# Silu on ScalarE for the gate, and six Strassen groups of inner columns instead of seven, spread over longer stretches

## The chip, the cores and the metric

The kernel runs on one core of a Trainium2 chip. The metric is device time in microseconds, as the median of three runs: 1667.15 us before the change, and the three runs lay between 1666.97 and 1667.17 us. TensorE (PE) multiplies matrices into PSUM, with a separate weight load before each matmul (PEld). VectorE (DVE) and ScalarE (ACT) do elementwise work, each in the order in which its instructions stand. SyncE (SP) issues the DMA transfers that bring the weights.

## What is computed

One decoder layer in fp32 with 256 tokens and a model width of 2048: two token mixers side by side, then a feed-forward part whose inner width is 5632.

```python
D_FF = ((8 * D_MODEL // 3 + 255) // 256) * 256          # 5632, eleven groups of 512
...
h = h + mixed @ w_out[l]
hn = rmsnorm(h, norm2_w[l])
h = h + (jax.nn.silu(hn @ w_gate[l]) * (hn @ w_up[l])) @ w_down[l]
return rmsnorm(h, norm_f_w)
```

`silu(z)` is `z * sigmoid(z)`. The change concerns only the line with `silu`: the gate, up and down projections.

## The kernel before

**Three products for one.** Every fp32 operand is split into a rounded part and a remainder, `hi` and `lo`, and a product is computed as `hi*hi + lo*hi + hi*lo`. For each weight tile ACT writes `hi` (line 169) and DVE subtracts it from the raw tile to get `lo` (line 170). So each weight that PE uses has passed ACT and DVE first.

**Units.** The work is a list of units, each with one weight tile. A plain unit (lines 300 to 331) loads 128x2048 numbers, 1 MB, and makes 24 matmuls with 512 columns at line 315. A pair unit (`strassen`, lines 334 to 385) loads 128x1024 numbers, 0.5 MB, of which DVE makes three more slots by subtraction (lines 187 to 189); ACT and DVE split seven slots, 128x1792, and PE makes 21 matmuls with 256 columns at line 362. This is Strassen's scheme with seven products in place of eight. It saves PE columns and costs DVE work.

**Groups.** The inner width is cut into eleven groups of 512 columns. A plain group is eight plain units: four for the gate (`wg`) and four for the up projection (`wu`). A Strassen group is sixteen pair units: eight for the gate (`sg`) and eight for up (`su`). Each set of eight pair units sums into the four PSUM banks of the pool `sp`, and `finish` (lines 374 to 383) forms the result `Z` out of them with one ACT copy and four DVE additions (lines 376 to 382). `PLAIN` (line 44) lists four plain groups, and the other seven are Strassen groups.

**Gate, up and turn.** When a gate's sums are ready, ACT takes the sigmoid (line 1160) and DVE multiplies it by the scaled gate (line 1161), for each of two token chunks. When up is ready, DVE multiplies by it (line 1165). Then `turn` transposes the product on PE (line 1180), and ACT and DVE split it into `f` (lines 1183, 1184), which is the operand of the down projection.

**Down.** Four parts, `PARTS`, take three, three, three and two groups. A part's four column blocks are twelve plain units (eight in the last part), `wd`; DVE adds their sums to `y` (line 1222).

**Order.** `ROW` (line 49) is a list of steps. Each names a main list of plain units (a plain group, or a down part) and the Strassen groups whose pair units `spread` (line 402) lays between the main units, evenly, with none behind the last `tail` main units. Only the last step with Strassen units has a tail, of 3. `run_units` (line 205) goes through the list, loads up to three units ahead, and there are three `hi` and `lo` buffers and four raw buffers in this phase (`WBUFS`, line 53, and one more each from line 1060). The DVE order is that of the program from unit 30 on (`manual_schedule`, line 1260). PE and ACT are reordered by the scheduler when the program is built, so parts of neighbouring units can change places there.

Of the kernel before, what the change touches and what calls it, by code (L numbers as in the profile page):

```python
# [9 lines left out]
AF = mybir.ActivationFunctionType  # L10
ALU = mybir.AluOpType
# [29 lines left out]
DLY, STEP = 1, 2  # L41

PARTS = [(0, 3), (3, 6), (6, 9), (9, 11)]
PLAIN = [0, 2, 5, 8]
NGRP = 11
STD = [4 * g + i for g in PLAIN for i in range(4)]
SGRP = [4 * g for g in range(NGRP) if g not in PLAIN]

ROW = [(("group", 0), [1]), (("group", 2), [3]), (("down", 0), [4]), (("group", 5), [6]), (("down", 1), [7]),
       (("group", 8), [9]), (("down", 2), [10]), (("down", 3), [])]  # L50


WBUFS = dict(raw=3, hi=2, lo=2)
# [13 lines left out]
def kernel(  # L67
# [991 lines left out]
    with tc.tile_pool(name="ffn", bufs=1) as ffn:  # L1059
# [92 lines left out]
        def group(g):  # L1152

            H = {}

            def gate(c, z):
                if c == 0:
                    H["sg"] = ffn.tile([P, 4, S], F32, tag="sg", name=f"sg_g{g}", bufs=2)
                v = H["sg"][:, 2 * c:2 * c + 2]
                A_.activation(v, z, AF.Sigmoid, scale=rt2[:, c:c + 1])  # L1160
                V.scalar_tensor_tensor(out=v, in0=z, scalar=rt2[:, c:c + 1], in1=v, op0=ALU.mult, op1=ALU.mult)

            def up(c, z):
                v = H["sg"][:, 2 * c:2 * c + 2]
                V.scalar_tensor_tensor(out=v, in0=z, scalar=rt2[:, c:c + 1], in1=v, op0=ALU.mult, op1=ALU.mult)
                if c == NC - 1:
                    if may_turn(g):
                        after(1, turn)
                    else:
                        turns.append((g, turn))  # L1170

            def turn():
                fh, fl = get_f(part_of[g])
                sg = H["sg"].rearrange("p a b -> p (a b)")
                for m in range(2):
                    ps = ps_unit(f"ptr_g{g}_{m}")
                    for i in range(2):
                        f = (2 * m + i) * P
                        for c in range(NC):
                            PE.transpose(out=ps[:, i * S + c * P:i * S + (c + 1) * P],  # L1180
                                         in_=sg[:, 2 * c * S + f:2 * c * S + f + P], identity=ident)
                    j = 4 * (g - PARTS[part_of[g]][0]) + 2 * m
                    A_.activation(flat(fh[:, j:j + 2]), ps, AF.Copy)
                    V.tensor_tensor(out=flat(fl[:, j:j + 2]), in0=ps, in1=flat(fh[:, j:j + 2]).bitcast(F32),  # L1184
                                    op=ALU.subtract)
                turned.append(g)
            return gate, up
# [21 lines left out]
            return (strassen(wst[i, 0], (hh, hl, sh, sl), z_tiles, f"sg{g}", then(gate, False)) +  # L1209
                    strassen(wst[i, 1], (hh, hl, sh, sl), z_tiles, f"su{g}", then(up, True)))  # L1210

        def down(pi):
            g0, g1 = PARTS[pi]

            def operand(g):
# [3 lines left out]
            def evac(q):  # L1219
# [14 lines left out]
                        downs[0] += 1  # L1234
                        run_turns()
                return fn
            for q in range(4):
                token_major_tiles(lambda g, q=q: wdown[4 * q:4 * q + 4, :, 512 * g:512 * g + 512], operand,
                                  range(g0, g1), f"wd{pi}_{q}", evac(q), ps_unit, by_chunk=(pi == last and q == 3))

        def listed(make):
            n = len(units)
            make()
            got = units[n:]
            del units[n:]
            return got
# [2 lines left out]
        dgf = ffn.tile([P, NC, P], F32, name="dgf")  # L1249
        for f in range(KT):  # L1250
            feature_major(wout[f], KT, mh, ml, f"wo{f}", wo_evac(f))
        for (kind, n), sides in ROW:
            main = listed(lambda: (plain_group if kind == "group" else down)(n))
            units.extend(spread(main, sum((strassen_group(g) for g in sides), []), 0, 3 if NGRP - 1 in sides else 0))
        find_free()
        load_next()
        with tc.issue_after(mm["last"]):
# [116 lines left out]
```

## Time and profile before

| | |
|---|---|
| median of three runs | 1667.15 us |
| profiled execution | 1667.3 us |
| its span, first to last instruction | 1665.5 us |
| granted TensorE clock | 0.997 of 2.4 GHz over the span |
| first matmul of the first plain group | 915.6 us |
| first matmul of the first down part | 1091.6 us |
| last sums leave, output part begins | 1652.4 us |

The feed-forward part thus takes 736.8 us of the span, and everything before 915.6 us has the same instructions on PE before and after. In the profile "busy" of an engine is the time in which some instruction of it is on record. Matmuls overlap, and a matmul's record lasts longer than the distance to the next one's start, so PE can be on record as busy through a short stall. The distance between starts in a long run of equal matmuls is the better measure of what PE needs.

The steps of `ROW` are told below by the time at which PE starts each step's first plain matmul: 915.6, 999.7, 1091.6, 1201.5, 1288.2, 1402.4 and 1489.9 us. They are called the first to the seventh old stretch. Stretches 1, 2, 4 and 6 have a plain group of eight main units, stretches 3, 5 and 7 a down part of twelve. The last down part stands behind the seventh, to 1652.4 us; in the windows below the two are divided at 1595 us.

### The profile page before, as it was taken

The numbers are of one execution on the slowest core, as the hardware profiler recorded it, in microseconds if no ns is written. First come the engines' busy times: TensorE is split into PE (matmuls) and PEld (weight loads), VectorE is DVE, ScalarE is ACT, GpSimd is POOL, SyncE is SP. The second block draws the span as 40 slices with busy tenths as digits, with TensorE's granted clock in tenths as the row PEclk, the third lists the DMA queues.
The fourth block names the chain that finished last, engine by engine and source line by source line (L and its number), as shares of the span: only waits on it lengthen the run. The fifth ranks groups of instructions, "written<-read, shape, count | busy, mean of one in ns | idle before, by whom it ended". The sixth has DMA issues, their size and how long they took to land. (4 is left out here: it accounts for less than half of the span.)

```text
span 1665.5 us, 27170 instructions
## 1 busy us (share of the span) xinstructions
PE 1631.2 (98%) x11370; PEld 1464.4 (88%) x11370; DVE 1345.8 (81%) x1734; ACT 831.3 (50%) x824; POOL 30.6 (2%) x64
## 2 busy tenths in 40 slices
PE   7999999999999999999999999999999999999998
PEld 6987899988998889988899998888888888888887
DVE  7797468887888878776665998998988989889974
ACT  5664444445544545444465654544544445544542
POOL 0000000000000000000000000000000000000000
PEclk8999999999999999999999999999999999999999
DMA  7545453555645555354673564655655565555671
GB/s 268 177 152 174 155 193 127 169 182 171 215 131 179 186 179 192 134 172 151 242 260 131 169 210 148 197 191 193 208 172 177 195 202 180 186 181 187 194 248 51
DMA packets 88540, 301.14 MB, mean 181 GB/s; under 512 B 6880, under 2 KB 11232, under 8 KB 72672
## 3 DMA queue, kind: packets, MB, share of 16 engines
q1 hardware_dynamic: 86976, 295.31, 53.5%
q10 hardware_dynamic: 1440, 4.08, 0.7%
q8 instruction: 89, 1.46, 0.4%
q14 instruction: 35, 0.29, 0.0%
HBM read 297.27 MB, written 2.10 MB: 180 GB/s over the span
## 5 line engine op out<-in xcount | busy, mean ns | idle before, releaser
L169 ACT ACTIVATE hi_t<-raw_t 128x2048 fp32r<-128x2048 f32 (+1 forms) x100 | 183.0, 1831 | 205.0 <-PE ps_t L287 101.7
L170 DVE TENSOR_TENSOR lo_t<-raw_t,hi_t 128x2048 fp32r<-128x2048 f32 (+1 forms) x100 | 217.7, 2181 | 60.0 <-ACT hi_t L169 42.1
L286 PE MATMUL ps_t<-hi_t,uh 128*128 128x512 f32 x480 | 190.7, 397 | 0.5 <-DVE gs L874 0.5
L287 PE MATMUL ps_t<-hi_t,ul 128*128 128x512 f32 x480 | 188.6, 393 | 0.0
L315 PE MATMUL ps_wd<-hi_wd,f 128*128 128x512 f32 x704 | 172.2, 392 | 1.5 <-DVE f L1184 1.1
L169 ACT ACTIVATE hi_sg<-raw_sg 128x1792 fp32r<-128x1792 f32 x56 | 95.0, 1698 | 122.4 <-DVE raw_sg L189 76.7
L315 PEld LDWEIGHTS ps_wd<-hi_wd,f 128*128 128x128 f32 x704 | 129.8, 188 | 28.6 <-ACT hi_wd L169 1.6
L169 ACT ACTIVATE hi_su<-raw_su 128x1792 fp32r<-128x1792 f32 x56 | 95.2, 1701 | 109.3 <-DVE raw_su L189 85.4
L170 DVE TENSOR_TENSOR lo_sg<-raw_sg,hi_sg 128x1792 fp32r<-128x1792 f32 x56 | 113.0, 2019 | 17.8 <-ACT hi_sg L169 17.8
L170 DVE TENSOR_TENSOR lo_su<-raw_su,hi_su 128x1792 fp32r<-128x1792 f32 x56 | 112.9, 2020 | 15.1 <-ACT hi_su L169 15.1
L291 PE MATMUL ps_t<-lo_t,uh 128*128 128x512 f32 x480 | 123.5, 395 | 0.0
L169 ACT ACTIVATE hi_wd<-raw_wd 128x2048 fp32r<-128x2048 f32 x44 | 84.1, 1912 | 54.0 <-PE ps_wd L315 19.4
L170 DVE TENSOR_TENSOR lo_wd<-raw_wd,hi_wd 128x2048 fp32r<-128x2048 f32 x44 | 100.5, 2285 | 12.6 <-ACT hi_wd L169 12.3
L286 PEld LDWEIGHTS ps_t<-hi_t,uh 128*128 128x128 f32 x480 | 90.2, 188 | 19.1 <-PE pst_t L362 0.9
L287 PEld LDWEIGHTS ps_t<-hi_t,ul 128*128 128x128 f32 x480 | 90.2, 188 | 17.7
L291 PEld LDWEIGHTS ps_t<-lo_t,uh 128*128 128x128 f32 x480 | 88.9, 188 | 18.1
L315 PE MATMUL ps_wd<-lo_wd,f 128*128 128x512 f32 x352 | 88.9, 393 | 1.2 <-DVE lo_wd L170 1.1
L315 PEld LDWEIGHTS ps_wd<-lo_wd,f 128*128 128x128 f32 x352 | 64.3, 188 | 14.6 <-DVE lo_wd L170 2.4
L235 PE MATMUL ps_v<-uh,hi_v 128*128 128x256 f32 x256 | 63.6, 286 | 0.6 <-DVE cb_v L501 0.6
L235 PE MATMUL ps_wo<-m,hi_wo 128*128 128x256 f32 x256 | 62.5, 285 | 0.8 <-ACT gs L872 0.8
L236 PE MATMUL ps_v<-ul,hi_v 128*128 128x256 f32 x256 | 63.2, 285 | 0.0
L236 PE MATMUL ps_r<-ul,hi_r 128*128 128x256 f32 x256 | 62.7, 284 | 0.0
(347 smaller groups left out, 3923.7 us busy)
## 6 DMA issues: line engine op xcount, KB each, us to landing
raw_t<-in_wtm_dram SPq DMA_DIRECT2D x60, 1024.0 KB, 4.9
raw_wd<-in_wdown_dram SPq DMA_DIRECT2D x44, 1024.0 KB, 5.2
raw_sg<-in_wst_dram SPq DMA_DIRECT2D x56, 512.0 KB, 3.6
raw_su<-in_wst_dram SPq DMA_DIRECT2D x56, 512.0 KB, 3.7
raw_t<-in_wsm_dram SPq DMA_DIRECT2D x40, 512.0 KB, 3.6
raw_v<-in_wqk_dram SPq DMA_DIRECT2D x16, 1024.0 KB, 4.9
raw_r<-in_wqk_dram SPq DMA_DIRECT2D x16, 1024.0 KB, 4.9
raw_wo<-in_wout_dram SPq DMA_DIRECT2D x16, 1024.0 KB, 4.9
```

The lines of the kernel that those rows point to most:

```text
L169: ia = A_.activation(hi[:, r], w[:, r], AF.Copy)
L170: iv = V.tensor_tensor(out=lo[:, r], in0=w[:, r], in1=hi[:, r].bitcast(F32), op=ALU.subtract)
L235: PE.matmul(o[0], hi[:, k * P:(k + 1) * P], ah[:, k, :], start=(k == 0), stop=False)
L236: PE.matmul(o[0], hi[:, k * P:(k + 1) * P], al[:, k, :], start=False, stop=False)
L286: PE.matmul(pst[c], uh[:, k, c * P:(c + 1) * P], w, start=(k == 0), stop=False)
L287: PE.matmul(pst[c], ul[:, k, c * P:(c + 1) * P], w, start=False, stop=False)
L291: PE.matmul(pst[c], uh[:, k, c * P:(c + 1) * P], lo[:, j * 512:(j + 1) * 512], start=False, stop=(k == KT - 1))
L315: PE.matmul(pst[c], u[:, k, c * P:(c + 1) * P], w[:, k], start=(start and k == 0 and q == 0), stop=(stop and k == 3))
```

## The change

The gate's sigmoid and multiplication become one activation. Group 10 becomes a plain group, so there are five plain and six Strassen groups. The steps of `ROW` may now hold several main lists: the first step has two plain groups and one Strassen group, the second and third each a down part, a plain group and two Strassen groups, the fourth a down part with a plain group in front of its last block and one Strassen group, and the last is the last down part alone. Every step now has a tail of 3.

```diff
-PLAIN = [0, 2, 5, 8]
+PLAIN = [0, 2, 5, 8, 10]
...
-ROW = [(("group", 0), [1]), (("group", 2), [3]), (("down", 0), [4]), (("group", 5), [6]), (("down", 1), [7]),
-       (("group", 8), [9]), (("down", 2), [10]), (("down", 3), [])]
+ROW = [([("group", 0), ("group", 2)], [1]), ([("down", 0), ("group", 5)], [3, 4]), ([("down", 1), ("group", 8)], [6, 7]),
+       ([("down", 2, (0, 1, 2)), ("group", 10), ("down", 2, (3,))], [9]), ([("down", 3)], [])]
...
-                A_.activation(v, z, AF.Sigmoid, scale=rt2[:, c:c + 1])
-                V.scalar_tensor_tensor(out=v, in0=z, scalar=rt2[:, c:c + 1], in1=v, op0=ALU.mult, op1=ALU.mult)
+                A_.activation(v, z, AF.Silu, scale=rt2[:, c:c + 1])
...
-        def down(pi):
+        def down(pi, blocks=range(4)):
...
-            for q in range(4):
+            for q in blocks:
...
-        for (kind, n), sides in ROW:
-            main = listed(lambda: (plain_group if kind == "group" else down)(n))
-            units.extend(spread(main, sum((strassen_group(g) for g in sides), []), 0, 3 if NGRP - 1 in sides else 0))
+        for mains, sides in ROW:
+            main = listed(lambda: [(plain_group if kind == "group" else down)(*n) for kind, *n in mains])
+            units.extend(spread(main, sum((strassen_group(g) for g in sides), []), 0, 3))
```

By `spread` the first new step lays 16 pair units behind 13 of its 16 main units, the second and third lay 32 behind 17 of their 20, the fourth 16 behind 17 of its 20. Before, the plain groups had 16 behind 8, the down parts 16 behind 12 (the third 16 behind 9). Lines from 1161 on move up by one.

The first place is DVE in the fourth old stretch, where plain group 5 and Strassen group 6 reach their gates together. `Z_sg` is formed out of the four `pst_sg` banks, `lo_` are the splits, `raw_` a pair unit's subtractions:

```order
L1161 SCALAR_TENSOR_TENSOR sg_g_12207<-ps_wg_0_11862,rt_8323,sg_g_12207 128x512
L187 TENSOR_TENSOR raw_su_1_12210<-raw_su_1_12210 128x512
L188 TENSOR_TENSOR raw_su_1_12210<-raw_su_1_12210 128x256
L189 TENSOR_TENSOR raw_su_1_12210<-raw_su_1_12210 128x256
L170 TENSOR_TENSOR lo_su_0_12216<-raw_su_0_12177,hi_su_0_12215 128x1792
L378 TENSOR_TENSOR Z_sg_12240<-pst_sg_0_11897,s_sg_12241 128x512
L379 TENSOR_TENSOR Z_sg_12240<-pst_sg_2_11899,Z_sg_12240 128x256
L380 TENSOR_TENSOR Z_sg_12240<-pst_sg_3_11900,Z_sg_12240 128x512
L382 TENSOR_TENSOR Z_sg_12240<-pst_sg_1_11898,Z_sg_12240 128x512
L1161 SCALAR_TENSOR_TENSOR sg_g_12207<-ps_wg_1_11863,rt_8323,sg_g_12207 128x512
L1161 SCALAR_TENSOR_TENSOR sg_g_12249<-Z_sg_12240,rt_8323,sg_g_12249 128x512
L170 TENSOR_TENSOR lo_su_1_12255<-raw_su_1_12210,hi_su_1_12254 128x1792
```

In the changed kernel's second step, beside plain group 5, the gate of Strassen group 4 stands so on DVE:

```order
L170 TENSOR_TENSOR lo_su_0_11592<-raw_su_0_11556,hi_su_0_11591 128x1792
L378 TENSOR_TENSOR Z_sg_11616<-pst_sg_0_11271,s_sg_11617 128x512
L379 TENSOR_TENSOR Z_sg_11616<-pst_sg_2_11273,Z_sg_11616 128x256
L380 TENSOR_TENSOR Z_sg_11616<-pst_sg_3_11274,Z_sg_11616 128x512
L382 TENSOR_TENSOR Z_sg_11616<-pst_sg_1_11272,Z_sg_11616 128x512
L170 TENSOR_TENSOR lo_su_1_11628<-raw_su_1_11586,hi_su_1_11627 128x1792
```

Three of the multiplications at line 1161 lay around the four additions (a fourth follows a few rows further down), and none is left; the plain group's gate now falls at another place.

The second place is PE where a Strassen group goes over from its gate to its up units. Before, in the third old stretch with Strassen group 4, the last third of one down unit (`wd_2_0`) and two thirds of the next stand between the last gate unit `sg_7` and the first up unit `su_0`:

```order
L362 MATMUL pst_sg_1_10995<-lo_sg_7_11300,sh 128x256
L315 MATMUL ps_wd_2_0_11405<-lo_wd_2_0_11333,f_10185 128x512 x4
L315 MATMUL ps_wd_2_1_11406<-lo_wd_2_0_11333,f_10185 128x512 x4
L315 MATMUL ps_wd_2_0_11405<-hi_wd_2_1_11401,f_10185 128x512 x8
L315 MATMUL ps_wd_2_1_11406<-hi_wd_2_1_11401,f_10185 128x512 x8
L362 MATMUL pst_su_2_11439<-hi_su_0_11360,hh 128x256
```

In the new second step the unit list has, behind main unit 5, `sg_7` and `su_0` of Strassen group 3 one directly behind the other. Both use the four `pst` banks. On PE stands:

```order
L362 MATMUL pst_sg_2_10470<-lo_sg_7_10758,sh 128x256
L362 MATMUL pst_sg_1_10469<-lo_sg_7_10758,sh 128x256
L315 MATMUL ps_wd_1_0_10696<-hi_wd_1_2_10817,f_9993 128x512 x8
L315 MATMUL ps_wd_1_1_10697<-hi_wd_1_2_10817,f_9993 128x512 x8
L315 MATMUL ps_wd_1_0_10696<-lo_wd_1_2_10818,f_9993 128x512 x4
L315 MATMUL ps_wd_1_1_10697<-lo_wd_1_2_10818,f_9993 128x512 x4
L362 MATMUL pst_su_2_10862<-hi_su_0_10784,hh 128x256
```

and on DVE, which keeps the order of the list:

```order
L170 TENSOR_TENSOR lo_sg_7_10758<-raw_sg_7_10722,hi_sg_7_10757 128x1792
L170 TENSOR_TENSOR lo_su_0_10785<-raw_su_0_10752,hi_su_0_10784 128x1792
L187 TENSOR_TENSOR raw_su_1_10812<-raw_su_1_10812 128x512
L188 TENSOR_TENSOR raw_su_1_10812<-raw_su_1_10812 128x256
L189 TENSOR_TENSOR raw_su_1_10812<-raw_su_1_10812 128x256
L170 TENSOR_TENSOR lo_wd_1_2_10818<-raw_wd_1_2_10782,hi_wd_1_2_10817 128x2048
L378 TENSOR_TENSOR Z_sg_10842<-pst_sg_0_10468,s_sg_10843 128x512
L379 TENSOR_TENSOR Z_sg_10842<-pst_sg_2_10470,Z_sg_10842 128x256
```

The down unit `wd_1_2`, which the list has behind `su_0`, has moved in front of it on PE and not on DVE. In the kernel before, the list has a main unit between `sg_7` and `su_0` at every such place. The third new step has the same place with Strassen group 6.

ACT gets one table load (`ACT_TABLE_LOAD`), directly ahead of the first gate's two activations in the first step. No other load is added.

## Rows read from the trace of the kernel before

**Rows 1.** The page, part 1: busy us (share of the span) and instructions.
```profile
PE 1631.2 (98%) x11370; PEld 1464.4 (88%) x11370; DVE 1345.8 (81%) x1734; ACT 831.3 (50%) x824; POOL 30.6 (2%) x64
```

**Rows 2.** Windows: stretch, length, busy us (instructions) PE PEld DVE ACT POOL, clock, DMA.
```profile
915.60:999.70 84.10, 84.10 (x531) 76.27 (x530) 78.98 (x89) 51.36 (x43) 2.17 (x1) 1.00 0.58 188
999.70:1091.60 91.90, 87.79 (x547) 77.81 (x546) 84.45 (x93) 46.79 (x34) 0.00 (x0) 1.00 0.58 182
1091.60:1201.50 109.90, 108.82 (x649) 96.91 (x648) 97.92 (x103) 53.61 (x37) 0.00 (x0) 1.00 0.61 198
1201.50:1288.20 86.70, 83.81 (x511) 73.51 (x509) 76.86 (x84) 42.90 (x31) 0.00 (x0) 1.00 0.54 170
1288.20:1402.40 114.20, 112.11 (x669) 99.39 (x670) 101.71 (x106) 56.52 (x38) 0.00 (x0) 1.00 0.62 198
1402.40:1489.90 87.50, 84.06 (x510) 73.60 (x508) 77.95 (x86) 42.75 (x31) 0.00 (x0) 1.00 0.56 175
1489.90:1595.00 105.10, 102.22 (x618) 89.85 (x618) 97.03 (x103) 54.04 (x36) 0.00 (x0) 1.00 0.66 211
1595.00:1652.40 57.40, 56.16 (x253) 45.97 (x251) 30.48 (x29) 20.55 (x25) 0.55 (x1) 1.00 0.31 100
```

**Rows 3.** Windows of line 315 on PE: length, busy us (instructions), clock, DMA.
```profile
999.70:1091.60 91.90, 47.68 (x193) 1.00 0.58 182
1091.60:1201.50 109.90, 68.82 (x288) 1.00 0.61 198
915.60:1652.40 736.80, 442.25 (x1824) 1.00 0.57 183
```

**Rows 4.** Windows of line 362 on PE, the same columns.
```profile
915.60:1652.40 736.80, 304.16 (x2352) 1.00 0.57 183
```

**Rows 5.** The chain that ended last: start us, us, what.
```profile
1348.62 8.19 PE ps_wd L315 x36
...
1478.94 1.69 ACT hi_su L169
...
1480.65 2.02 DVE lo_su L170
...
1526.34 5.05 PE pst_sg L362 x42
...
1594.58 0.44 PE ptr_g L1180 x4
```

**Rows 6.** Waits, 940 to 1660 us: in total, times, longest us.
```profile
ACT hi_su L169 <- DVE raw_su L189: 85.4, 33, 3.8
ACT hi_sg L169 <- DVE raw_sg L189: 73.1, 22, 6.4
```

**Rows 7.** Groups by line and form, DVE, 900 to 1665 us: busy us, mean ns.
```profile
L170 DVE TENSOR_TENSOR lo_su<-raw_su,hi_su 128x1792 fp32r<-128x1792 f32 x56 | 112.9, 2020 | 15.1 <-ACT hi_su L169 15.1
...
L170 DVE TENSOR_TENSOR lo_wg<-raw_wg,hi_wg 128x2048 fp32r<-128x2048 f32 x16 | 36.5, 2284 | 2.5 <-PE pst_su L362 1.4 <-ACT hi_wg L169 1.2
...
L187 DVE TENSOR_TENSOR raw_su<-raw_su 128x512 f32<-128x512 f32 x56 | 38.3, 684 | 0.2 <-DMA raw_su<-in_wst_dram 0.2
...
L188 DVE TENSOR_TENSOR raw_su<-raw_su 128x256 f32<-128x256 f32 x56 | 23.8, 425 | 1.8
...
L1161 DVE SCALAR_TENSOR_TENSOR sg_g<-Z_sg,rt,sg_g 128x512 f32<-128x512 f32 x14 | 10.4, 748 | 1.6 <-ACT sg_g L1160 1.2
...
L1161 DVE SCALAR_TENSOR_TENSOR sg_g<-ps_wg,rt,sg_g 128x512 f32<-128x512 f32 x8 | 5.9, 744 | 0.0
...
L380 DVE TENSOR_TENSOR Z_sg<-pst_sg,Z_sg 128x512 f32<-128x512 f32 x7 | 4.8, 690 | 0.2
...
L379 DVE TENSOR_TENSOR Z_sg<-pst_sg,Z_sg 128x256 f32<-128x256 f32 x7 | 3.0, 424 | 0.6
```

**Rows 8.** The same for ACT; the table load is from the whole span.
```profile
L1160 ACT ACTIVATE sg_g<-Z_sg,rt 128x512 f32<-128x512 f32 x14 | 9.4, 716 | 10.9 <-DVE Z_sg L382 10.9
...
L509 ACT ACT_TABLE_LOAD x3 | 3.8, 1283 | 1.9 <-DVE cv_v L506 1.8
```

## The prediction

> **What bounds the kernel now.** The page comes first: PE is on record as busy for 98% of the span and DVE for 81% [rows 1]. A reader could stop there and call PE the bound, so that the change, which adds PE columns, must cost time. Both shares need a second look, stage by stage.
>
> The windows of the feed-forward part [rows 2] show that DVE is not at 81% there. In the second and the seventh stretch it is busy for 92% of the time (84.45 of 91.90 us, 97.03 of 105.10 us), and PE has idle time just there: 4.1 and 2.9 us. The first stretch has no PE idle time at all.
>
> How much PE really loses needs counts and paces. In runs of equal matmuls [rows 5] a plain matmul takes 8.19 / 36 = 0.2275 us, a pair unit's 5.05 / 42 = 0.1202 us, a transpose 0.44 / 4 = 0.11 us. From 915.6 to 1652.4 us stand 1824 plain [rows 3] and 2352 Strassen matmuls [rows 4], and the eight windows' PE counts [rows 2] add to 4288, or 4274 without the two on each of the seven boundaries that count twice, which leaves 98 others. PE's need is 415.0 + 282.7 + 10.8 = 708.5 us. The part takes 736.8 us, so PE stalls for 28.3 us. (The windows record 17.8 us of idle time, since a matmul's record covers the start of a stall.) In the second stretch the need is 193 x 0.2275 + 354 x 0.1202 = 86.5 us of 91.9, a stall of 5.4; in the third 288 x 0.2275 + 361 x 0.1202 = 108.9 us of 109.9, a stall of 1.0.
>
> What PE waits for is read from the chain [rows 5]: near 1480 us it runs through ACT `hi_su`, DVE `lo_su`, DVE `raw_su`, not through PE. ACT in turn waits for DVE's subtractions, 85.4 and 73.1 us in all [rows 6]. So where pair units are dense, DVE sets the pace, and elsewhere PE does.
>
> **The change part by part.**
>
> *Group 10 becomes plain.* PE loses 16 x 21 = 336 Strassen matmuls, 40.4 us, and gains 8 x 24 = 192 plain ones, 43.7 us: +3.3 us, on the path wherever PE is the bound. DVE [rows 7] loses 16 x (2.020 + 0.684 + 2 x 0.425) = 56.9 us and two gatherings of `Z`, each 3 x 0.690 + 0.424 = 2.5 us, and gains 8 x 2.284 = 18.3 us: -43.6 us. The weights are 8 MB either way. Where plain units follow one another PE takes 1 MB in 5.46 us, 192 GB/s, and the seventh stretch moved 211 with the DMA engines busy at 0.66 [rows 2]. So I price the transfers at nothing; a late one would cost PE what it is late.
>
> The Trainium skill, "TensorE: Matmul & The Clock Gate", section "Wait — 56ns, not 53.3ns?", gives a warm matmul's distance as its columns over 2.4 GHz and some 2.5 ns more. By it the two kinds would take 0.2158 and 0.1092 us, and the swap would cost 41.4 - 36.7 = 4.7 us, which would put the forecast 1.4 us higher. The rows show 0.2275 and 0.1202 us at full clock, some 11 ns more for either kind, and the measurement decides.
>
> *Silu.* DVE loses 22 multiplications, 14 x 0.748 + 8 x 0.744 = 16.4 us [rows 7]. ACT has no Silu in this trace. The nearest row is the sigmoid with the same shape and scale, 0.716 us [rows 8], and I take the same. If Silu took half as long or twice as long, 22 of them would move ACT by 8 or 16 us out of 369 busy in 736.8 us (the ACT column of rows 2 added up). ACT is half idle, so most of that stays hidden; I keep 2 us either way for the range. One table load of 1.283 us [rows 8] falls in the first stretch, the one without a PE stall, behind splits that are loaded ahead. If that cover were gone it would cost 1.3 us once.
>
> *Spreading.* Per plain unit PE needs 24 x 0.2275 = 5.46 us and DVE 2.284; per pair unit PE 21 x 0.1202 = 2.52 and DVE 3.55. Two pair units per plain unit, as in the old plain-group stretches, make 9.4 us of DVE on 10.5 of PE before any evacuation. The new first step has 16 / 13 = 1.23 pair units per plain unit, the fourth 0.94. These are far on PE's side, like the third old stretch with 1.33 and a 1.0 us stall, and I give them 0.5 and 1.0 us.
>
> The second and third new steps decide. Each holds exactly the kind and amount of work of the second and third old stretch together: DVE 84.45 + 97.92 = 182.4 us, PE 86.5 + 108.9 = 195.4 us. Without the multiplications of three gates (6 x 0.746) DVE is at 177.9. But the three last main units carry no pair units, so the 17 others hold 171.0 us of DVE (less 3 x 2.284) and 179.0 of PE (less 3 x 5.46), which is 95.5%. DVE busy over PE's need was 97.6% in the second old stretch, with a stall of 6.2% of the need, and 89.9% in the third, with 0.9%. A straight line between them gives 4.8% of 179.0 = 8.5 us per step. On the other side, at the rate of the third stretch it would be 1.7 us.
>
> I take 6 us, nearer to the upper end. Against the line speaks that the old stalls come in bursts. Where a plain group and a Strassen group reached their gates together, 4 x 0.746 + 2.5 = 5.5 us of DVE work stood between the splits; now 2.5 us stands there, away from the other gate, and the tail units let DVE get ahead before each new step. For the line speaks that 1.88 pair units per plain unit is hardly below 2, and that the turns, where DVE waits for PE's transposes, are as many as before.
>
> **The sum.** Stalls after: 0.5 + 6 + 6 + 1.0 + 1.2 (the end from 1595 us on, unchanged, 57.40 - 56.16 [rows 2]) = 14.7 us instead of 28.3, a gain of 13.6. The swap costs 3.3. Net -10.3 us. The profiled execution took 1667.3 us, 0.15 above the median of the runs, so I expect 1657 us.
>
> **The rivals.**
>
> *DVE falls away as the bound.* It loses 60 us of its 645 (the DVE column of rows 2 added up). If 95.5% is low enough, as the 93.9% of the first stretch was (78.98 us in 84.1, no idle PE), the two dense steps stall for 1 to 2 us each, and about 5 us in all remain: 1667.15 - 23.3 + 3.3 = 1647 us. Against it: the fourth and sixth stretches, at about the same share, lost 2.9 and 3.4 us of recorded PE time each.
>
> *The dense steps stay as they were.* If the stall belongs to the pair units and not to the total, the 5.4 us that went with 16 of them in the second stretch come four times: 21.6 + 2.7 = 24.3 us of stall, and the 4.0 us saved go for the swap. That gives 1667.15 - 4.0 + 3.3 = 1666.4 us, no change. For it: the pattern of two pair units to one plain unit is hardly changed there. Against it: the 4.5 us per step that Silu takes from DVE.
>
> *Slower: the banks between `sg_7` and `su_0`.* In the second and third new steps these follow one another directly in the list. `su_0` needs the four banks, and on DVE their gathering stands behind `lo_su_0`, three subtractions and `lo_wd_1_2`: 2.02 + 1.53 + 2.28, and the first two additions, 1.11 = 6.9 us [rows 7]. PE has one down unit in front of `su_0`, 5.46 us. If DVE starts on this row when `sg_7` ends, PE waits 1.5 us at each of the two places; if DVE is one pair unit late, 3.55 us more. On top of stalls that stay as they were that is 1669 to 1676 us, and I put it at 1671. It decides from the point where DVE reaches `lo_su_0` later than PE ends `sg_7`. Against it: DVE may do both splits while PE is still in `sg_7`.
>
> **How the numbers follow.** My forecast of partial relief, 1652 to 1664 us, gets 0.60; full relief, under 1652, 0.15; unchanged dense steps, 1664 to 1670, 0.18; the slower case 0.07. Differences of 0.2%, 3.3 us, can be told from no change: faster means under 1663.8, so 0.75; same 0.18; slower, above 1670.5, 0.07. The range of 8 in 10 reaches into both neighbours and takes in Silu's 2 us: 1649 to 1667 us.
>
> **What would show it right or wrong.** In the changed profile 2016 matmuls at line 362 and 2016 at line 315, at the same paces; about 585 us of DVE in the feed-forward part; 22 Silu activations near 0.7 us, and one more table load. Windows over the steps should show PE without idle time in the first and fourth, and a few us in each of the second and third, with DVE near 92% there. The waits of PE for `hi_` and `lo_` tiles should halve. I am wrong if the dense steps stall by 9 us or more each, if Silu takes much longer than the sigmoid, or if PE waits at `su_0` for DVE's `Z`.

## The result and the profile after

The changed kernel takes 1655.97 us (median of 4 runs, 1654.24 to 1657.85) against 1667.06 for the kernel before on the same chip: a ratio of 0.9935, 95% interval 0.9917 to 0.9952. That is 11.1 us faster, 1.0 us under the forecast of 1657. The mechanism turned out only partly as forecast: holding one engine to the program's order, with nothing else changed, proved to be worth 8.9 us more. The profiled execution is the fastest of the four, 1654.24 us, so the stalls read from it below are those of the best run and not of the median.

The page's first part answers to [rows 1]:

```profile
PE 1626.6 (98%) x11226; PEld 1459.9 (88%) x11226; DVE 1292.9 (78%) x1648; ACT 821.6 (50%) x815; POOL 35.0 (2%) x64
```

DVE lost 52.9 us of busy time where the prediction's durations add to 60.0. They overstate the cost, as neighbours overlap: in the trace of `e4_apart`, one of the experiments, a `lo_su` of 2.03 us starts at 1129.18 and the next row at 1131.12, 1.94 us later. For the same reason the feed-forward part still has 594 us of DVE (the DVE column below added up), where 585 were forecast.

The windows by step answer to [rows 2] (four steps with Strassen units, then the last down part, up to the first `po` product):

```profile
915.50:1048.40 132.90, 132.90 (x768) 117.28 (x767) 107.84 (x111) 73.66 (x61) 6.52 (x1) 1.00 0.58 190
1048.40:1244.10 195.70, 193.84 (x1179) 172.93 (x1178) 175.40 (x184) 99.86 (x68) 0.00 (x0) 1.00 0.60 194
1244.10:1443.50 199.40, 193.63 (x1171) 172.16 (x1170) 175.65 (x185) 99.11 (x68) 0.00 (x0) 1.00 0.59 188
1443.50:1575.90 132.40, 132.40 (x740) 116.02 (x739) 100.53 (x93) 62.48 (x40) 0.00 (x0) 1.00 0.64 206
1575.90:1639.40 63.50, 62.32 (x283) 51.14 (x282) 34.55 (x35) 23.80 (x28) 0.55 (x1) 1.00 0.30 100
```

The first and fourth steps have no idle PE time. The same two lines as in [rows 3, 4], for the second and third steps, give PE's need there, L315:

```profile
1048.40:1244.10 195.70, 116.28 (x481) 1.00 0.60 194
1244.10:1443.50 199.40, 113.93 (x480) 1.00 0.59 188
```

and L362:

```profile
1048.40:1244.10 195.70, 87.88 (x674) 1.00 0.60 194
1244.10:1443.50 199.40, 84.78 (x667) 1.00 0.59 188
```

At the paces of [rows 5] and with 24 transposes the second step needs 481 x 0.2275 + 674 x 0.1202 + 2.6 = 193.0 us, the third 192.0. They stall for 2.7 and 7.4 us (a window also counts the few matmuls that only reach into it, which makes these stalls up to half a microsecond too small). That is striking, for the two steps hold the same kinds of units in the same order. Over the whole part PE needs 2016 x 0.2275 + 2016 x 0.1202 + 10.8 = 711.7 us, and it takes 1639.3 - 915.5 = 723.8, so 12.1 us of stall remain of 28.3. In the table further down, "stall" is this figure.

Silu answers to [rows 8] (columns: minimum, median and maximum in ns), and the waits to [rows 6]:

```profile
L1160 ACT ACTIVATE sg_g<-Z_sg,rt x12: 704/709/730, 979.1 to 1517.1; 128x512 f32<-128x512 f32 x12
L1160 ACT ACTIVATE sg_g<-ps_wg,rt x10: 667/682/692, 947.2 to 1542.1; 128x512 f32<-128x512 f32 x10
L1160 ACT ACT_TABLE_LOAD  x1: 1283/1283/1283, 945.9 to 945.9; - x1
```

```profile
ACT hi_sg L169 <- DVE raw_sg L189: 68.9, 21, 6.4
ACT hi_su L169 <- DVE raw_su L189: 47.7, 19, 4.5
```

Silu costs what the sigmoid cost, with one load. ACT still waits for the subtractions, but only the wait of `hi_su` has fallen much (from 85.4; that of `hi_sg` from 73.1, with a seventh fewer pair units).

Why does the third step stall more than the second? Here is the largest single stall, on ACT, DVE and PE in turn (start, duration, in brackets the idle time before and what ended it):

```profile
1362.38 1.92 ACT L169 ACTIVATE hi_wg<-raw_wg 128x2048 fp32r<-128x2048 f32 x1 [2.92 <-DMA raw_wg<-in_wgate_dram]
1364.21 1.68 ACT L169 ACTIVATE hi_sg<-raw_sg 128x1792 fp32r<-128x1792 f32 x1
1365.79 1.06 ACT L1182 ACTIVATE f<-ptr_g 128x512 fp32r<-128x512 f32 x2
1369.55 1.70 ACT L169 ACTIVATE hi_sg<-raw_sg 128x1792 fp32r<-128x1792 f32 x1 [2.70 <-issue]
```

```profile
1360.88 0.42 DVE L189 TENSOR_TENSOR raw_sg<-raw_sg 128x256 f32<-128x256 f32 x1
1361.23 2.02 DVE L170 TENSOR_TENSOR lo_sg<-raw_sg,hi_sg 128x1792 fp32r<-128x1792 f32 x1
1365.92 2.02 DVE L170 TENSOR_TENSOR lo_sg<-raw_sg,hi_sg 128x1792 fp32r<-128x1792 f32 x1 [2.67 <-ACT hi_sg L169]
...
1369.04 0.42 DVE L189 TENSOR_TENSOR raw_sg<-raw_sg 128x256 f32<-128x256 f32 x1
1369.38 2.28 DVE L170 TENSOR_TENSOR lo_wg<-raw_wg,hi_wg 128x2048 fp32r<-128x2048 f32 x1
```

```profile
1365.94 0.62 PE L362 MATMUL pst_sg<-hi_sg,hh 128*128 128x256 f32 x3 [0.75 <-ACT hi_sg L169]
...
1371.30 0.62 PE L362 MATMUL pst_sg<-hi_sg,hh 128*128 128x256 f32 x3 [2.21 <-ACT hi_sg L169]
```

ACT stands still for 2.92 us for the transfer of plain unit `wg8_0`. Behind it waits the `hi` half of pair `sg7_5`, whose raw tile DVE had finished at 1361.3 and which DVE and PE both need first. DVE loses 2.67 us, PE 0.75 and then 2.21. The second of PE's waits comes by way of DVE: being late, it ends the next pair's subtractions only at 1369.46, and ACT starts that pair's `hi` at 1369.55 (the view calls ACT's wait there "issue"). The Trainium skill, "PSUM — Partial Sum Buffer", section "Engine vs sequencer instructions", calls the queues of ScalarE and VectorE strictly first in, first out; these rows agree, since the ready `hi_sg` did not pass the waiting `hi_wg`. The order of the built program shows how it came to this, ACT first, then DVE:

```
615 L169 ACTIVATE hi_wg8_0_13134<-raw_wg8_0_13099 128x2048
616 L169 ACTIVATE hi_sg7_5_13101<-raw_sg7_5_13069 128x1792
...
1268 L170 TENSOR_TENSOR lo_sg7_5_13102<-raw_sg7_5_13069,hi_sg7_5_13101 128x1792
1272 L170 TENSOR_TENSOR lo_wg8_0_13135<-raw_wg8_0_13099,hi_wg8_0_13134 128x2048
```

DVE follows the program, ACT the order that the scheduler chose. I call it a reversal where two successive `lo` halves on DVE have their `hi` halves in the opposite order on ACT. The changed kernel has 18: 4 in the second step, 12 in the third and 2 in the fourth. So the step with three times the reversals has nearly three times the stall; that they cause it is not shown by this count.

### The profile page after: what moved, and what is told of

It reads as the page before. It is cut to its first block, busy times and chain, and to the rows that moved or that the text cites. A ratio compares the mean times of both kernels' runs of the same rounds, so it can differ in the third digit from the quotient of the medians.

```text
span 1652.5 us, 26750 instructions
## 1 busy us (share of the span) xinstructions
PE 1626.6 (98%) x11226; PEld 1459.9 (88%) x11226; DVE 1292.9 (78%) x1648; ACT 821.6 (50%) x815; POOL 35.0 (2%) x64
## 4 chain that ended last, share of the span: by engine, by line
PE 91%; DVE 4%; DMA 3%; ACT 1%; issue 1%; SPq 0%; POOL 0%; ACTq 0%; DVEq 0%
PE ps_wd L315 12%; PE pst_su L362 7%; PE ps_t L286 7%; PE ps_t L291 7%; PE ps_t L287 7%; PE ps_wu L315 7%; PE ps_wg L315 6%; PE pst_t L362 6%; PE pst_sg L362 5%; PE ps_v L236 2%; PE ps_v L235 2%; PE ps_r L235 2%; PE ps_v L238 2%; PE ps_r L236 2%; PE ps_wo L235 2%; PE ps_wo L236 2%
## 5 line engine op out<-in xcount | busy, mean ns | idle before, releaser
L315 PE MATMUL ps_wd<-hi_wd,f 128*128 128x512 f32 x704 | 170.6, 391 | 1.0 <-DVE f L1183 1.0
L315 PEld LDWEIGHTS ps_wd<-hi_wd,f 128*128 128x128 f32 x704 | 129.9, 188 | 27.0 <-DVE f L1183 1.2
L169 ACT ACTIVATE hi_sg<-raw_sg 128x1792 fp32r<-128x1792 f32 x48 | 81.6, 1702 | 118.5 <-DVE raw_sg L189 68.9
L169 ACT ACTIVATE hi_su<-raw_su 128x1792 fp32r<-128x1792 f32 x48 | 81.6, 1699 | 85.2 <-DVE raw_su L189 47.7
L170 DVE TENSOR_TENSOR lo_su<-raw_su,hi_su 128x1792 fp32r<-128x1792 f32 x48 | 97.0, 2022 | 32.4 <-ACT hi_su L169 15.3
L170 DVE TENSOR_TENSOR lo_sg<-raw_sg,hi_sg 128x1792 fp32r<-128x1792 f32 x48 | 96.9, 2021 | 16.8 <-PE ps_wd L315 7.8
L287 PEld LDWEIGHTS ps_t<-hi_t,ul 128*128 128x128 f32 x480 | 90.2, 188 | 17.7
L315 PE MATMUL ps_wd<-lo_wd,f 128*128 128x512 f32 x352 | 88.6, 391 | 3.4 <-DVE lo_wd L170 3.4
L315 PEld LDWEIGHTS ps_wd<-lo_wd,f 128*128 128x128 f32 x352 | 64.8, 188 | 16.8 <-DVE lo_wd L170 4.0
L315 PE MATMUL ps_wg<-hi_wg,hh 128*128 128x512 f32 x160 | 62.8, 392 | 0.3 <-ACT hi_wg L169 0.3
```

The source lines that it names most:

```text
L169: ia = A_.activation(hi[:, r], w[:, r], AF.Copy)
L170: iv = V.tensor_tensor(out=lo[:, r], in0=w[:, r], in1=hi[:, r].bitcast(F32), op=ALU.subtract)
L287: PE.matmul(pst[c], ul[:, k, c * P:(c + 1) * P], w, start=False, stop=False)
L315: PE.matmul(pst[c], u[:, k, c * P:(c + 1) * P], w[:, k], start=(start and k == 0 and q == 0), stop=(stop and k == 3))
```

## The experiments

All twelve, with the two kernels of the change. Reversals are counted in the built order, and the order of the starts in the traces gives the same counts; stall is worked out as above (PE's need is 708.5 us with seven Strassen groups, 711.7 with six), and ratios are to the kernel before on the same chip:

| kernel | Strassen groups, plan | gate | time, us | ratio, 95% interval | reversals | stall, us |
|---|---|---|---|---|---|---|
| before | 7, short | sigmoid | 1667.1 | 1 | 24 | 28.3 |
| e1_silu | 7, short | Silu | 1657.34 | 0.9941 (0.9929 to 0.9954) | 22 | 18.7 |
| e8_swap_old | 6, short | Silu | 1659.75 | 0.9956 (0.9943 to 0.9968) | 19 | 17.2 |
| changed | 6, long | Silu | 1655.97 | 0.9935 (0.9917 to 0.9952) | 18 | 12.1 |
| e2_mult | 6, long | sigmoid | 1663.44 | 0.9978 (0.9969 to 0.9988) | 18 | 21.0 |
| e3_seven | 7, long | Silu | 1668.45 | 1.0005 (0.9996 to 1.0014) | 19 | 28.6 |
| e4_apart | 6, long, 2 per unit | Silu | 1653.79 | 0.9918 (0.9904 to 0.9931) | 11 | 12.2 |
| e5_even | 6, even | Silu | 1646.17 | 0.9875 (0.9861 to 0.9888) | 6 | 3.7 |
| e7_even_mult | 6, even | sigmoid | 1650.50 | 0.9902 (0.9888 to 0.9915) | 14 | 7.6 |
| e6_even7 | 7, even | Silu | 1654.05 | 0.9920 (0.9907 to 0.9934) | 19 | 14.8 |
| e9_act_order | 6, long | Silu | 1647.06 | 0.9880 (0.9867 to 0.9894) | 0 | 5.4 |
| e10_before_act_order | 7, short | sigmoid | 1654.86 | 0.9927 (0.9914 to 0.9941) | 0 | 15.9 |
| e11_even7_act_order | 7, even | Silu | 1652.29 | 0.9912 (0.9899 to 0.9926) | 0 | 12.8 |
| e12_even6_act_order | 6, even | Silu | 1647.23 | 0.9884 (0.9867 to 0.9900) | 0 | 4.8 |

**The parts of the change.** `e1_silu` is the kernel before with the one gate edit, `e2_mult` the changed kernel without it:

```diff
-                A_.activation(v, z, AF.Sigmoid, scale=rt2[:, c:c + 1])
-                V.scalar_tensor_tensor(out=v, in0=z, scalar=rt2[:, c:c + 1], in1=v, op0=ALU.mult, op1=ALU.mult)
+                A_.activation(v, z, AF.Silu, scale=rt2[:, c:c + 1])
```

> The kernel before with Silu in place of Sigmoid and multiplication, and nothing else: seven Strassen groups, the old stretches. VectorE loses 22 multiplications of 0.746 us, 16.4 us. Theory (VectorE sets the pace in the stretches that carry Strassen units): of the 28 us in which TensorE stands still in the feed-forward part, the multiplications of the seven Strassen groups come off, 7 x 1.49 = 10.4 us at the most, and about half of it where some stretches were not paced by VectorE: 1661 us, range 1657 to 1665. Rival (TensorE waits for hi and lo pieces, whose order of arrival the multiplications do not set): 1667 us, no change. By the theory the new plan and the swap are then worth some 5 us of the 11; by the rival all of them.

Measured 1657.34 us: 9.8 us for Silu alone, nearly the theory's upper bound of 10.4. The rival's time falls. The second, fourth and sixth stretches answer to [rows 2]:

```profile
1000.20:1089.80 89.60, 87.45 (x539) 78.25 (x538) 80.85 (x87) 47.12 (x34) 0.00 (x0) 0.98 0.59 187
1198.80:1282.90 84.10, 82.72 (x511) 73.40 (x509) 74.07 (x80) 42.94 (x31) 0.00 (x0) 1.00 0.57 176
1397.20:1481.60 84.40, 82.90 (x510) 73.35 (x509) 74.08 (x80) 42.91 (x31) 0.00 (x0) 1.00 0.56 175
```

They take 258.1 us instead of 266.1 (about 1 us of it because the first window has eight matmuls fewer), and PE's idle time in them falls from 10.4 to 5.0 us. Yet the reversals are the same in both kernels, none, six and six. So the multiplications on DVE cost time there, and not by way of reversals.

> The changed kernel with Sigmoid and multiplication back, its plan kept (six Strassen groups, long stretches). VectorE gets 16.4 us back, of which some 5 us fall in each of the second and third steps (two Strassen groups and one plain group at 1.49 us each). Theory (these two steps are near VectorE's limit, the first and fourth are not): up to 4.5 us more stall in each of the two, nothing elsewhere: 1662 us, range 1659 to 1666. Rival (the plan alone did it): 1656 us as the changed kernel. Rival (the table load or Sigmoid against Silu matter): below 1656.

Measured 1663.44: as the theory had it, also by place. The second step takes 200.6 us and the third 203.4, which is 4.9 and 4.0 more than in the changed kernel, and the first and fourth take what they took (some 1.7 us of the third step's 4.0 are TensorE's clock, by an estimate as in the last section). The second step has four reversals in both kernels. Swap and plan without Silu are worth 3.7 us.

`e8_swap_old` adds only the swap to `e1_silu`:

```diff
-ROW = [...
-       (("group", 8), [9]), (("down", 2), [10]), (("down", 3), [])]
+ROW = [...
+       ([("group", 8)], [9]), ([("down", 2, (0, 1, 2)), ("group", 10), ("down", 2, (3,))], []), ([("down", 3)], [])]
```

> The swap alone: Silu, the old short stretches, group 10 computed as a plain group between the third and fourth column blocks of the third down part, which then carries no pair units. Against the kernel before with Silu (1657.3 us) TensorE does 3.3 us more by the rows' paces, and the stall of the stretch that carried group 10 (2.5 us in that kernel's trace) goes. Theory: 1658 us, range 1656 to 1660, so that the even spreading is worth 1 to 2 us of the change. Rival (group 10 by Strassen cost VectorE 43.6 us that held up other stretches too): 1653 us. Rival (a plain group costs TensorE more than its matmuls, by its transposes and evacuations): 1661 us or more.

Measured 1659.75, inside the theory's range. The swap by itself loses 2.4 us: PE does 3.2 us more and stalls 1.5 less, which makes 1.7; the rest is not explained. Spreading then gives 3.8 (1659.75 to 1655.97).

`e3_seven` keeps long stretches but not the swap:

```diff
-PLAIN = [0, 2, 5, 8, 10]
+PLAIN = [0, 2, 5, 8]
+ROW = [([("group", 0), ("group", 2)], [1, 3]), ([("down", 0), ("group", 5)], [4, 6]), ([("down", 1), ("group", 8)], [7, 9]),
+       ([("down", 2)], [10]), ([("down", 3)], [])]
```

> The changed kernel with group 10 by Strassen again (seven Strassen groups), in long stretches (two groups with 32 pair units; first down part and a group with 32; second down part and a group with 32; third down part with 16), Silu kept. Against the changed kernel TensorE does 3.3 us less and VectorE 43.6 us more, which falls into the first stretch (32 pair units over 13 main units, 2.5 each) and the fourth (16 over 9). Theory (VectorE paces where pair units stand dense): the first stretch stalls for 6 to 10 us, the fourth for 1 to 2: 1656 - 3.3 + 9 = 1662 us, range 1658 to 1666. Rival (long stretches are what helps, the swap only costs TensorE): 1653 us. The kernel before with Silu alone took 1657.3 us with the same seven groups in short stretches.

Measured 1668.45, 6 us slower than the theory and outside its range. The crowded first stretch, here as two windows, alone has 5.0 and 3.3 us of recorded idle PE time, and its stall is larger, since a matmul's record covers the start of one:

```profile
914.80:1016.50 101.70, 96.71 (x624) 88.06 (x623) 94.03 (x110) 58.95 (x51) 2.17 (x1) 0.99 0.53 173
1016.50:1098.90 82.40, 79.14 (x461) 69.89 (x461) 70.75 (x72) 42.74 (x30) 0.00 (x0) 0.97 0.59 189
```

Part of the miss is TensorE's clock: three times, 3.4 us each, this run was granted half of it (the last section has the rows), which cost some 4.4 us by an estimate from the paces, 3.0 of them in the first stretch. With this plan the swap is worth 12.5 us, some 4 of them clock, with the old one -2.4. It has no price of its own.

**Place or density.** `e4_apart` puts two pair units behind each of 16 main units in the dense steps:

```diff
-            units.extend(spread(main, ..., 0, 3))
+            units.extend(spread(main, ..., 0, 2 + len(sides)))
```

> The changed kernel with exactly two pair units behind each main unit of the second and third steps (16 main units carry them, not 17), so that a down unit stands between the last unit of sg and the first of su. Theory A (the place where sg ends and su begins at once costs the 1.5 and 2.2 us that TensorE waits there for the lo half of the down unit): these two waits go, 1652 us. Theory B (density decides: 2.0 pair units for a main unit, not 1.88, so VectorE is at 98% of TensorE's time and not at 95.5%): the two waits go, but the other units of the steps wait 2 to 4 us more in each step, 1658 to 1660 us.

Measured 1653.79. PE's two waits for `lo_wd` are gone, as theory A had it, but neither theory explains the two dense steps, the second and the third:

```profile
1049.90:1250.50 200.60, 193.59 (x1157) 171.62 (x1156) 173.47 (x184) 97.27 (x68) 0.00 (x0) 0.99 0.60 186
1250.50:1442.40 191.90, 191.90 (x1171) 172.12 (x1170) 175.35 (x182) 100.80 (x69) 0.00 (x0) 1.00 0.64 200
```

The same units take 8.7 us longer the first time. In the third step PE is never idle, with DVE busy for 91% of it and the pair units closer than in the changed kernel. So DVE's load at this density does not force the stall. What is known to differ is the order on ACT: 10 of the kernel's 11 reversals stand in the second step, none in the third. PE's longest wait in the second step, 3.22 us, is for DVE's `y`; DVE came to it late after 1.69 us of waiting for the `hi_sg` of a reversed pair.

**An even plan.** `e5_even` joins steps in pairs; `e7_even_mult` is the same without Silu:

```diff
+ROW = [([("group", 0), ("group", 2), ("down", 0), ("group", 5)], [1, 3, 4]),
+       ([("down", 1), ("group", 8), ("group", 10), ("down", 2)], [6, 7, 9]), ([("down", 3)], [])]
```

> The changed kernel with its first two steps joined into one (48 pair units over 36 main units) and its third and fourth too (48 over 40), six Strassen groups and Silu kept. The work of each engine is the same; no main unit is followed by more than two pair units, and 1.45 and 1.3 stand for one main unit on average where the dense steps had 1.88. VectorE has 7.3 us of work in each 9.1 us of TensorE's. Theory (the stall sits in steps with too many pair units for VectorE): of the 14 us of stall in the feed-forward part some 10 go, 1646 us, range 1643 to 1650. Rival (the stall comes from places, such as the end of sg and the turn of a group, of which there are as many as before): 1653 to 1656. Rival (buffers of the gate and up halves are held longer, TensorE waits for them): above 1656.

Measured 1646.17, as the theory had it, and the lowest median of all: 20.9 us under the kernel before and 9.8 under the changed one. But the plan also cut the reversals from 18 to 6, so it does not tell density from order.

> The even plan with six Strassen groups (1646.2 us), with Sigmoid and multiplication back in place of Silu: VectorE gets 22 multiplications of 0.746 us, 16.4 us, and is at about 85% of TensorE's time in the joined stretches. Silu was worth 9.8 us in the old plan and 7.5 us in the changed one. Theory (VectorE's work costs only where pair units stand dense): 1 to 2 us, 1648 us, range 1646 to 1649. Rival (the multiplication delays the turn of each group, or the gate's buffers, wherever it stands): 7 us or more, 1653 us.

Measured 1650.50, between the two: Silu still gives 4.3 us where DVE has room. The multiplication also moved ACT's order (14 reversals, not 6), so the 4.3 us cannot be put down to load alone.

`e6_even7` has seven Strassen groups in two even stretches (the two numbers in each step are its pair units and its tail; the pair units left over go into the next step):

```diff
+PLAIN = [0, 2, 5, 8]
+ROW = [([("group", 0), ("group", 2), ("down", 0), ("group", 5)], [1, 3, 4, 6], 60, 0),
+       ([("down", 1), ("group", 8), ("down", 2)], [7, 9, 10], 52, 3), ([("down", 3)], [], 0, 3)]
```

> Seven Strassen groups and Silu in two even stretches: 60 pair units over 36 main units, then 52 over 32 (the units of group 6 cut between them). Against the even plan with six groups (1646.2 us) TensorE does 3.3 us less and VectorE 43.6 us more, but no main unit carries more than two pair units: 1.7 and 1.8 on average, VectorE at 91 and 93% of TensorE's time by durations. Theory (the stall comes with density, little of it below 95%): 2 to 4 us more stall against 3.3 us less work, 1646 us, range 1643 to 1650. Rival (the stall grows evenly with VectorE's load: 43.6 us more of it bring 10 us back): 1653 us. Rival (below its limit VectorE costs nothing at all): 1643 us.

Measured 1654.05. My theory failed; the rival by which 43.6 us of DVE work bring 10 us back was right in size: 11.1 us more stall for 3.2 us less work.

**The order by itself.** Four kernels differ from before, changed, `e6_even7` and `e5_even` in one line each:

```diff
-        with tc.manual_schedule(engines={nc.vector.engine}):
+        with tc.manual_schedule(engines={nc.vector.engine, nc.scalar.engine}):
```

> The changed kernel with ScalarE's instructions of the feed-forward part issued in the order in which the program is written, as VectorE's are already, instead of in the scheduler's order. In the changed kernel ScalarE makes the hi half of a later unit before that of an earlier one, whose hi VectorE needs first, 18 times (4 in the second step, 12 in the third, 2 in the fourth); here never. Theory C (the order of the two engines against each other makes the stalls: in the kernel with two pair units behind each main unit the second step, with 10 such reversals, stalls 10 us and the third, of the same units with none, not at all): some 10 of the 14 us go, 1646 us, range 1643 to 1651. Theory of the prediction (VectorE at 95% of TensorE's time in the dense steps makes them): no change, 1656 us. Rival (ScalarE's other work in the written order, squares and turns, now stands in front of hi halves): above 1658 us.

Measured 1647.06: 8.9 us less, with every instruction of the changed kernel kept. The profiled executions lie 7.2 us apart, and 6.7 of that is stall; the rest of the 8.9 is that the changed kernel's other runs were slower than its profiled one. The dense steps:

```profile
1047.70:1241.60 193.90, 193.32 (x1178) 173.09 (x1177) 175.69 (x184) 99.51 (x69) 0.00 (x0) 1.00 0.63 196
1241.60:1434.20 192.60, 191.06 (x1157) 170.58 (x1155) 175.25 (x184) 98.51 (x69) 0.00 (x0) 1.00 0.63 199
```

DVE is as busy as in the changed kernel, and PE's idle time falls from 1.9 and 5.8 us to 0.6 and 1.5. In the changed kernel's two dense steps ACT waited for transfers like this, and in this kernel's the list of waits has no such row:

```profile
ACT hi_wd L169 <- DMA raw_wd<-in_wdown_dram: 13.6, 8, 1.9
ACT hi_wg L169 <- DMA raw_wg<-in_wgate_dram: 5.0, 3, 2.9
ACT hi_wu L169 <- DMA raw_wu<-in_wup_dram: 2.0, 2, 1.8
```

This shows that ACT's order makes more than half of the stall that the change left, 6.7 of 12.1 us. The edit holds all of ACT's work to the program, copies, squares and Silu too, so the reversals of the halves are the likely part of it and not one tested alone.

> The kernel before with ScalarE's instructions of the feed-forward part in the written order, and nothing else: Sigmoid and multiplication, seven Strassen groups, short stretches. It has 24 reversals between ScalarE's and VectorE's order, and 28 us of stall. Theory C (the reversals make the stalls, some 0.7 to 1 us each): 15 to 20 us go, 1649 us, range 1645 to 1655. Theory of the prediction (VectorE's load paces the stretches, which this does not change): 1665 to 1667 us. If both act: 1655 to 1662 us, as VectorE is at 96% and more of TensorE's time in some stretches.

Measured 1654.86: 12.3 us from the one line, more than the whole change gave, without touching the arithmetic or the plan. The time lies at the end of theory C's range and just under the "both act" one; the stretches speak for "both act": two down stretches run with no idle PE, the three plain-group stretches still lose 2 to 3 us each.

```profile
999.70:1090.50 90.80, 87.59 (x546) 78.18 (x545) 84.60 (x93) 46.55 (x34) 0.00 (x0) 1.00 0.58 184
1090.50:1199.20 108.70, 108.70 (x649) 96.70 (x648) 98.60 (x104) 54.01 (x37) 0.00 (x0) 1.00 0.61 200
1199.20:1286.50 87.30, 85.11 (x531) 76.40 (x530) 81.92 (x88) 45.90 (x32) 0.00 (x0) 1.00 0.59 186
1286.50:1395.20 108.70, 108.70 (x650) 96.70 (x648) 98.32 (x104) 53.66 (x37) 0.00 (x0) 1.00 0.61 200
1395.20:1482.70 87.50, 85.03 (x531) 76.33 (x530) 81.90 (x88) 45.89 (x32) 0.00 (x0) 1.00 0.59 184
```

There DVE is busy for 93 to 94% of the time, against 90 to 91% in the down stretches. The first of these rows took 91.9 us in the kernel before [rows 2], where it had no reversal either. Load does matter, then, as `e1_silu` showed, but the share alone does not say when: the first stretch has DVE busy for 94% and PE never idle [rows 2].

> Seven Strassen groups in two even stretches, with Silu (1654.1 us), and ScalarE's instructions in the written order. It had 19 reversals and 11 us more stall than the even plan with six groups (6 reversals, 1646.2 us), though TensorE has 3.3 us less to do. Theory C: the 11 us go, 1641 us, range 1639 to 1646: the seventh Strassen group pays once the order is right. Theory of the prediction (43.6 us more on VectorE cost 8 to 11 us): 1654 us.

Measured 1652.29: only 1.8 us less, though all 19 reversals are gone, so they were not what held the seventh group back, unless the written order takes back elsewhere what it gives: ACT waits 52.5 us for the transposes of the turns, where it waited 9.6. It comes nearer to the prediction's theory, 1654, than to mine, 1641.

> The even plan (six Strassen groups, Silu) with ScalarE in the written order too: both remedies at once. The even plan alone took 1646.2 us with 6 reversals, the written order alone (in the changed kernel's plan) 1647.1 us with none. Theory (both remove the same stall of some 9 us; what is left is mostly the two places at the end, the last turn and the last product, 1.2 and 0.4 us): 1645 us, range 1643.5 to 1646.5. Rival (they remove different stalls and add up): below 1642 us. Rival (ScalarE, in order, now waits for the transposes of a turn with hi halves behind it): 1647 to 1650 us.

Measured 1647.23, no gain over `e5_even` (1646.17, 1645.42 to 1647.16). In the written order ACT waits longer for the transposes of the turns, with `hi` halves behind it (first this kernel, then `e5_even`):

```profile
ACT f L1182 <- PE ptr_g L1179: 56.0, 11, 7.0
```

```profile
ACT f L1182 <- PE ptr_g L1179: 17.7, 8, 4.2
```

The time is in the second rival's range and above the theory's, and these waits are the ones that this rival names. Of the changed kernel's 12.1 us of stall the even plan alone took 8.4 and the written order alone 6.7, together more than there were, so at least 3 us are the same stall. Whether the rest is too, or the new waits eat up a gain, is not shown. With no reversals, six groups against seven in the even plan are worth 5.1 us (1652.29 to 1647.23): 8.0 us less stall for 3.2 us more work. There the swap pays without any help from the order. DVE's load is the candidate: with seven groups the two stretches of `e11_even7_act_order` have DVE at 89 and 91%.

```profile
915.20:1273.80 358.60, 354.56 (x2166) 317.39 (x2166) 320.78 (x341) 191.66 (x143) 1.37 (x1) 1.00 0.60 190
1273.80:1590.30 316.50, 313.92 (x1915) 280.68 (x1914) 288.12 (x303) 160.48 (x110) 0.00 (x0) 1.00 0.61 198
```


## Why the prediction was right, and where not

*The bound.* PE, with stalls where pair units are dense: right. The stall is in the windows, not in PE's share, and 16.2 of its 28.3 us went. PE's recorded waits for `hi_` and `lo_` tiles from 915 to 1650 us fell from 15.7 to 7.5 us, half, as forecast.

*The swap.* PE's +3.3 us was right (711.7 against 708.5), and so were counts and paces. DVE's relief was put too high, 60 us instead of 52.9. "I price the transfers at nothing" was wrong in the third step, where a transfer 2.92 us late cost PE 0.75 and 2.21 us. The forecast that DVE's relief pays for it holds with the spreading, not without (`e8_swap_old`).

*Silu.* Duration, count and one table load were as forecast, and the table load stayed hidden. What was mis-sized is its worth. The prediction gave it 4.5 us of DVE per step and no figure of its own; by itself it is 9.8 us in the old plan and 7.5 in the new. Per dense step the 4.5 us were near: 4.9 and 4.0 (`e2_mult`, with the clock in the second).

*Spreading.* The first and fourth steps: 0.5 and 1.0 us forecast, no idle PE time measured. The second and third were put at 6 us each, with DVE near 92%; 2.7 and 7.4 were measured, with DVE at 90 and 88%. The sum was close, but the step behind it failed: a straight line through DVE's share in two old stretches. The 7.4 us are not DVE at its limit, since with ACT in written order the same units leave PE idle for 0.6 and 1.5 us instead of 1.9 and 5.8 (`e9_act_order`), and two steps of the same units and load lie 8.7 us apart in `e4_apart`. The prediction named ACT `hi_` as a link of the chain, then priced only DVE. That its 6 us per step came out near the mean of the two, 5, is luck: ACT's order supplied most of a stall that it had put down to load.

*The sum.* Stall 14.7 forecast, 12.1 measured (the 17.8 us of recorded idle time before should be 17.7); net -10.3 against -13.0 between the two profiled spans (1665.5 and 1652.5) and -11.1 between the medians.

*The rivals.* Full relief (1647 us) was not reached, though `e9_act_order` and `e5_even` show that it was there to be had. Unchanged dense steps fell. The place between `sg_7` and `su_0` was real, once in each dense step:

```profile
1099.45 0.73 PE L315 MATMUL ps_wd<-lo_wd,f 128*128 128x512 f32 x2 [1.37 <-DVE lo_wd L170]
...
1295.66 1.20 PE L315 MATMUL ps_wd<-lo_wd,f 128*128 128x512 f32 x4 [2.00 <-DVE lo_wd L170]
```

That is near the 1.5 us at each that the rival priced, but PE waits for `lo_wd_1_2`, one unit earlier than the forecast `Z`, and the other stall did not stay as it was. The wait for `Z` that it forecast does show where it was not looked for: in `e3_seven` PE waits up to 1.9 us at an `su` unit for DVE's `Z_sg`, in `e5_even` up to 1.3.

Three things stay open: how Silu's worth divides where the edit also moved ACT's order, above all its 4.3 us in the even plan; whether the reversals or the rest of ACT's order made the stall that `e9_act_order` and `e10_before_act_order` took away; and why seven groups stall for 12.8 us in the even plan without reversals. Another order for ACT (the turns' copies later, `hi` halves in DVE's order) was not tried.

## What to carry to other kernels

Where two in-order engines prepare halves of the same tile, compare their orders before you blame the load of either: a reversal puts a late transfer in front of a ready tile. Two stretches of the same units with different stalls are the sign to look for. Load still costs where the order is right. And a change of plan or of duration also changes what a scheduler does with the engines left to it, so measure the parts alone, each with the order held.

## What was unexpected of the hardware

A wait of PE can cost more than itself. In `e4_apart` PE stood idle for 3.22 us up to 1182.96, ran at full clock for a moment, and was then granted half of it, the 1.2 GHz level, before it came back (the last three columns: granted clock, DMA share, GB/s):

```profile
1178.60:1182.60 4.00, 1.10 (x7) 0.90 (x7) 3.93 (x5) 2.08 (x2) 0.00 (x0) 1.00 0.75 227
1182.90:1184.40 1.50, 1.44 (x6) 1.22 (x7) 1.50 (x4) 0.00 (x0) 0.00 (x0) 1.00 0.66 168
1184.40:1187.80 3.40, 3.40 (x9) 2.69 (x9) 3.33 (x5) 1.70 (x1) 0.00 (x0) 0.50 0.22 89
1187.80:1190.00 2.20, 2.20 (x11) 1.76 (x10) 1.96 (x4) 0.55 (x1) 0.00 (x0) 0.99 0.48 168
```

In those 3.40 us PE started 8 matmuls (the ninth of the row only reaches in), where at 0.2275 us it starts 15. That is about 1.6 us on top of the wait, and the row counts them as busy. In `e3_seven` half clock came three times, after idle times of 2.43, 1.95 and 2.20 us:

```profile
1014.79:1018.20 3.41, 3.41 (x15) 3.02 (x14) 3.34 (x5) 1.70 (x1) 0.00 (x0) 0.50 0.75 286
1048.92:1052.34 3.42, 3.42 (x16) 3.42 (x17) 3.21 (x7) 1.34 (x2) 0.00 (x0) 0.50 0.59 184
1226.41:1229.83 3.42, 3.42 (x15) 3.03 (x14) 1.57 (x3) 0.60 (x1) 0.00 (x0) 0.50 0.55 158
```

It does not follow every such wait. In `e1_silu` the fall came behind 1.72 us of idle time; the kernel before has the same wait of 1.72 us at the same place and kept its full clock, and so did the changed kernel behind its 2.21 us. So the stalls of `e1_silu`, `e2_mult`, `e4_apart` and `e6_even7` in the table hold one such stretch each, that of `e3_seven` three, and the others none.

The table load cost its own 1.283 us and nothing more: it ran from 945.94, and the first Silu started at 947.23. The Trainium skill, "ScalarE: Activation LUTs", section "What ACT_TABLE_LOAD costs", adds a drain of about 1.38 us to the same 1283 ns; this trace shows none behind the load.

The time of the changed kernel also varied more from run to run, by 3.6 us, than with ACT in written order, by 0.3 us (`e9_act_order`). That waiting for transfers in the wrong order also passes their variation on to PE would fit, and so would a clock that fell in some of the runs: the changed kernel's four runs, from the fastest to the slowest, were granted 0.998, 0.997, 0.996 and 0.996 of it over the span, and all four of `e9_act_order` 0.998. Neither was shown.
